# Two weight tiles moved ahead of the last head's products, branch tiles split by GpSimd alone, and output loads under an order block

## The chip, the cores and the metric

The kernel runs on one core of a Trainium2 chip. The time is the device time of one execution in microseconds; the kernel before took 1817.15 us (median of three runs, 1814.82 to 1818.39). One execution was taken by the hardware profiler; its trace is the source of every other time.

The core has five engines, each with its own queue that it works off in order: TensorE (PE, with its weight loads PEld), VectorE (DVE), ScalarE (ACT), GpSimd (POOL) and SyncE (SP, which here only issues transfers). An instruction that waits for a semaphore holds up all that stands behind it on its engine.

## What is computed

Two layers of a small transformer with adaptive norms: 256 tokens of width 2048 (and 256 context tokens) go through a Fourier mixing layer and then an attention layer, whose branch is 4096 wide. The change lies in the second layer, from its attention on:

```python
def _attention_branch(h, hc, w_in, sink, rows, cols, need_ctx):
    q, k, v, z = jnp.split(h @ w_in, [D_BRANCH, D_BRANCH + kvw, D_BRANCH + 2 * kvw], axis=-1)
    ...
    o = lax.map(block, ...)          # softmax(q k + mask, sink) v, 64 heads on 8 key heads
    ...
    y = jnp.moveaxis(o, 0, 1).reshape(b, n, D_BRANCH) * jax.nn.silu(z)
...
    x = x + gate * (y @ w_out[i])
    ...
return _rmsnorm(x, final_g)
```

## The kernel before

Products are done in split single precision: a matrix is kept as a rounded high part and the low rest, and one product is three TensorE instructions, high by high, high by low, low by high (`mm3`, lines 78 to 80). So every weight tile that is loaded (`raw`, 1 MB, three buffers, on SP's queue, line 49) is split before use: ScalarE casts the high part (line 65), VectorE subtracts it from the tile (line 66), in halves of 1024 columns (`half_split`; six buffers).

**Heads and weight units.** The attention stage is one loop over i = 0 to 65. Step i issues the scores of head i (`stage_s`, lines 1154 and 1155; 64 heads, two blocks of 128 tokens each), one weight unit (`filler`), the value product of head i − 2 (`stage_o`, lines 1176 and 1177) and a second weight unit. A weight unit is half of a 1 MB tile or of a query tile: queries of later heads ("q"), gates ("z", 32 of them in two halves, lines 1118 and 1120), and last, 12 units "o" of the output product.

After the scores, VectorE adds the mask and takes the row maximum (line 1156), ScalarE the exponential (line 1159), and the softmax is written as an fp16 pair `f` by ScalarE and VectorE (lines 1166, 1167; three buffers). Two DMA transposes on SP's queue (line 1168) turn it into `ft`, which the value product reads. ScalarE and VectorE take the result out of PSUM (lines 1182, 1183), and `emit_y` multiplies it by the gate (line 1139) into `y1`, 32 branch blocks of 256 columns (half a tile each).

**The output product.** `y @ w_out` is done in three parts by columns: 512 columns (`oA`, weights `wo1a`, 16 half tiles), 1024 (`wo1b`, 16 tiles) and 512 (`wo1c`). Before it can be used, a branch block is split into high and low like the weights (`y_split`): ScalarE casts, and for blocks 0 to 23 GpSimd subtracts, for blocks 24 to 31 VectorE. Blocks 0 to 15 are written into the buffers of the layer's input `hx1`, which are free once the last z unit has read them, 16 to 23 into `act` buffers, and 24 to 31 into a pool `fin`, which opens when the attention's pool has closed. `o1_step` does two token blocks of one branch block, calling `y_split` up to four blocks ahead. The 12 "o" units cover blocks 0 to 23 of the first part; blocks 24 to 31 follow after the loop, then part two with its own four PSUM banks, then part three.

**The output's inputs.** After the loop GpSimd's queue (line 1223 on) loads the gate `gbc` (1 MB), the residual `x2` out of the scratch tensor `x1d` (eight pieces of 256 KB) and the final gain `fg` (1 MB). `evac` (lines 1239 to 1244) needs them when part one is complete.

**What sets the order.** The instructions are written in program order, and a scheduler reorders each engine's queue at build time by its own estimate of durations; the pools and semaphores are added by the same build. `tc.issue_after(ins)` adds order edges to `ins` from those instructions of its block that are on the engine of `ins`; it adds no wait.

Of the kernel before, what the change touches and what calls it, by code (L numbers as in the profile page):

```python
# [31 lines left out]
def tile_dit(ctx: ExitStack, tc: tile.TileContext, a: dict, out: bass.AP):  # L32
# [10 lines left out]
    def psum():  # L43
        return pp.tile([P, 512], F32, tag="ps", name="ps")
# [842 lines left out]
    with tc.tile_pool(name="h1", reuse_waits="tile", bufs=16) as h1p:  # L887
# [72 lines left out]

        y1 = []
        raw1, fin = [None], []
        oA, kg1, yh = [], [0], []
        with tc.tile_pool(name="at", reuse_waits="tile", bufs=2) as at:

            kk, qq, obs, szs = {}, {}, {}, {}
# [113 lines left out]
            def emit_unit():  # L1080
                if pos[0] >= len(ulist):
                    return
                u = ulist[pos[0]]
                if pos[0] not in ready:
                    ready[pos[0]] = prep(u)
                if pos[0] + 1 < len(ulist):
                    ready[pos[0] + 1] = prep(ulist[pos[0] + 1])
                w = ready.pop(pos[0])
                pos[0] += 1
                kind, n, i, o = u  # L1090
                if kind == "o":
                    if n == 0:
                        oA.extend([psum(), psum()])
                    for j in range(2):
                        o1_step(n * 2 + j, oA, *(t[:, j * 512 : (j + 1) * 512] for t in w))
                    return
                wh, wl = w
                if kind == "q":
                    if i == 0:
                        o += [psum(), psum()]  # L1100
                    if (n, i) == (0, 4):
                        with tc.issue_after(last_cast[0]):
                            prep_kk(0)
                    for j in range(2):
                        k = i * 2 + j
                        q = slice(j * 512, (j + 1) * 512)
                        for tb in range(2):
                            mm3(o[tb], hx1[k][:, tb * P : (tb + 1) * P], hx1[k][:, N + tb * P : N + (tb + 1) * P], wh[:, q], wl[:, q], k == 0, k == KT - 1)
                    if i == 7:
                        finish_q(n, o)  # L1110
                else:
                    if i == 0:
                        o.append(psum())
                    for k in range(i * 8, i * 8 + 8):
                        q = slice((k % 8) * P, (k % 8 + 1) * P)
                        for part in (0, 1) if k < KT - 1 else (1, 0):
                            if part == 0:
                                PE.matmul(o[0], wh[:, q], hx1[k], start=k == 0, stop=k == KT - 1)  # L1118
                            else:
                                PE.matmul(o[0][:, 0:N], wl[:, q], hx1[k][:, 0:N], start=False, stop=False)  # L1120
                    if i == 1:
                        th = at.tile([P, N], F32, tag="th", name="th", bufs=3)
                        zs = at.tile([P, N], F32, tag="zs", name="zs", bufs=1)
                        S.copy(zs, o[0][:, N : 2 * N])
                        V.tensor_tensor(zs, o[0][:, 0:N], zs, op=ALU.add)
                        S.activation(th, zs, AF.Tanh, scale=0.5)
                        V.scalar_tensor_tensor(th, th, 1.0, zs, op0=ALU.add, op1=ALU.mult)
                        szs[n] = th
                        emit_y(n)
# [3 lines left out]
            def emit_y(blk):  # L1133
                if blk not in szs or (blk, 1) not in obs or blk in ydone:
                    return
                ydone.add(blk)
                if blk % 2 == 0:
                    y1.append(act())
                V.scalar_tensor_tensor(y1[blk // 2][:, (blk % 2) * N : (blk % 2 + 1) * N], obs[blk, 1], dsc[:, blk // 4 : blk // 4 + 1], szs.pop(blk), op0=ALU.mult, op1=ALU.mult)

            def stage_s(i):
                hk, blk, hh = i // 8, i // 2, i % 2
# [21 lines left out]
                for tb in range(2):  # L1164
                    f = at.tile([P, 1024], F16, tag="f", name="f", bufs=3)
                    S.activation(f[:, 0:512], pt[tb], AF.Copy, scale=sm[:, tb : tb + 1])  # L1166
                    V.scalar_tensor_tensor(f[:, 512:1024], pt[tb], sm[:, tb : tb + 1], f[:, 0:512], op0=ALU.mult, op1=ALU.subtract)  # L1167
                    nc.sync.dma_start_transpose(ft[:, :, tb, :], f)
                return ft

            def stage_o(i, ft):
# [36 lines left out]
            for i in range(66):  # L1208
# [11 lines left out]
        with tc.tile_pool(name="fin", reuse_waits="tile", bufs=1) as fp:  # L1220
            fin.append(fp)
            gbc = fp.tile([P, D], F32, name="gbc")
            nc.gpsimd.dma_start(gbc, gated.broadcast_to([P, D]))
            x2 = []
            for tb in range(2):
                x2.append([act() for _ in range(4)])
                for c in range(4):
                    nc.gpsimd.dma_start(x2[tb][c], x1d[tb, :, c * 512 : (c + 1) * 512])
            fg = fp.tile([P, D], F32, name="fg")
            nc.gpsimd.dma_start(fg, a["fg"].broadcast_to([P, D]))  # L1230
            ss = fp.tile([P, 9], F32, name="ss")

            sum_end = [None]
# [15 lines left out]
                    o1_step(k + i, oA, *(t[:, i * 512 : (i + 1) * 512] for t in w))  # L1249
            for tb in range(2):  # L1250
                evac(tb, 0, oA[tb])
            o = [[psum() for _ in range(2)] for _ in range(2)]
            for kg in range(16):
                w = ws_split(raw(a["wo1b"][kg]))
                for j in range(2):
                    k = kg * 2 + j
                    wh, wl = w[j]
                    for tb in range(2):
                        for c in range(2):
                            q = slice(c * 512, (c + 1) * 512)  # L1260
                            mm3(o[tb][c], yh[k][:, tb * P : (tb + 1) * P], yh[k][:, N + tb * P : N + (tb + 1) * P], wh[:, q], wl[:, q], k == 0, k == NB - 1)
# [173 lines left out]
```

## Time and profile before

| | |
|---|---|
| median of three runs | 1817.15 us |
| profiled execution | 1817.29 us |
| its span | 1815.5 us |
| TensorE busy | 1768.6 us (97%) |
| VectorE busy | 1412.0 us (78%) |
| ScalarE busy | 896.9 us (49%) |
| GpSimd busy | 212.4 us (12%) |
| mean granted TensorE clock | 0.993 |
| attention stage, first value product to last | 1172 to 1659 us |

How to read the rows further down: a row of the time order has start, duration, engine, line, operation, result `<-` operands and count, and in brackets how long the engine stood idle before it and what ended that. A row of a group has count, busy time, mean nanoseconds of one, and idle time before. Matmuls are pipelined, so their durations overlap; the distance of two starts is what one costs. Shares over the whole span average over stages with different limits.

### The profile page before, as it was taken

What the parts mean: (1) busy time and instruction counts of PE and PEld (TensorE: products, weight loads), DVE (VectorE), ACT (ScalarE), POOL (GpSimd) and SP (SyncE); (2) the same over time, 40 slices, a digit from 0 to 9 for tenths busy, and PEclk for the clock granted to TensorE, in tenths of its full rate; (3) what the DMA queues carried; (4) which work ended last, traced back from release to release, by engine and by line L of the source; (5) the groups of instructions that cost most, each with busy time, mean ns of one, the idle gap of its engine ahead of it and who ended that gap; (6) DMA issues with size and microseconds to landing.
All of it is one profiled execution on the core that took longest, in us unless ns stands there. A gap on an engine that the chain in (4) does not pass through costs nothing. (4 is left out here: it accounts for less than half of the span.)

```text
span 1815.5 us, 25987 instructions
## 1 busy us (share of the span) xinstructions
PE 1768.6 (97%) x9417; PEld 1480.2 (82%) x9417; DVE 1412.0 (78%) x2759; ACT 896.9 (49%) x1540; POOL 212.4 (12%) x213
## 2 busy tenths in 40 slices
PE   6999999999999999999999999999999999997998
PEld 4679999888888888888888888788878888875886
DVE  5679888786878887776875654899999999985455
ACT  5545454532222233324322534687778888874343
POOL 0001122100000000000001000402302231161001
PEclk9999999999999999999999999999999999998999
DMA  9988889665767647663567323587988888986553
GB/s 395 417 331 234 231 239 255 216 228 224 252 228 262 244 168 295 229 237 121 186 230 293 119 93 116 162 206 196 224 203 195 215 223 211 213 219 194 188 182 139
DMA packets 209472, 399.91 MB, mean 220 GB/s; under 512 B 156288, under 2 KB 156688, under 8 KB 174272
## 3 DMA queue, kind: packets, MB, share of 16 engines
q1 hardware_dynamic: 185280, 360.24, 61.7%
q0 software_dynamic: 19920, 31.06, 7.0%
q10 hardware_dynamic: 4144, 6.95, 1.1%
q8 instruction: 74, 1.21, 0.3%
q14 instruction: 54, 0.44, 0.1%
HBM read 352.06 MB, written 12.59 MB: 201 GB/s over the span
## 5 line engine op out<-in xcount | busy, mean ns | idle before, releaser
L65 ACT CAST wh<-raw 128x1024 fp32r<-128x1024 f32 x333 | 348.7, 1048 | 531.9 <-PE ps L79 431.1
L66 DVE TENSOR_TENSOR wl<-raw,wh 128x1024 fp32r<-128x1024 f32 x333 | 430.5, 1296 | 220.1 <-ACT wh L65 217.7
L79 PE MATMUL ps<-act,wh 128*128 128x512 f32 x1024 | 398.2, 389 | 0.0
L78 PE MATMUL ps<-act,wh 128*128 128x512 f32 x1024 | 393.8, 389 | 0.0
L80 PE MATMUL ps<-act,wl 128*128 128x512 f32 x1024 | 392.9, 389 | 0.0
L80 PEld LDWEIGHTS ps<-act,wl 128*128 128x128 f32 x1024 | 192.3, 188 | 39.8
L79 PEld LDWEIGHTS ps<-act,wh 128*128 128x128 f32 x1024 | 192.3, 188 | 39.8
L78 PEld LDWEIGHTS ps<-act,wh 128*128 128x128 f32 x1024 | 192.3, 188 | 39.7
L1118 PE MATMUL ps<-h,wh 128*128 128x512 f32 x512 | 185.5, 398 | 0.0
L686 DVE CUSTOM_DVE_ANT_0 raw<-raw,cb 128x512 f32<-128x512 f32 x256 | 172.4, 688 | 11.6 <-DMA raw<-in_adw 8.0
L686 DVE CUSTOM_DVE_ANT_0 junk<-raw,cb 128x512 f32<-128x512 f32 x192 | 131.8, 686 | 32.8 <-DMA raw<-in_adw 21.9
L1120 PE MATMUL ps<-h,wl 128*128 128x256 f32 x512 | 138.9, 281 | 0.0
L79 PE MATMUL ps<-wl,h 128*128 128x512 f32 x320 | 127.1, 397 | 0.4 <-DVE wl L66 0.4
L80 PE MATMUL ps<-wh,h 128*128 128x512 f32 x320 | 125.3, 395 | 0.0
L78 PE MATMUL ps<-wh,h 128*128 128x512 f32 x320 | 124.0, 402 | 0.0
L1167 DVE SCALAR_TENSOR_TENSOR f<-p,sm,f 128x512 f16<-128x512 f32 x128 | 102.9, 821 | 16.4 <-ACT f L1166 16.0
L1118 PEld LDWEIGHTS ps<-h,wh 128*128 128x128 f32 x512 | 96.6, 189 | 19.1
L1166 ACT ACTIVATE f<-p,sm 128x512 f16<-128x512 f32 x128 | 88.1, 717 | 41.5 <-DMA ft<-f 21.6
L1159 ACT ACTIVATE p<-ps,mx 128x512 f32<-128x512 f32 x128 | 87.9, 688 | 38.1 <-DVE mx L1156 31.6
L1120 PEld LDWEIGHTS ps<-h,wl 128*128 128x128 f32 x512 | 97.0, 190 | 2.8
L1156 DVE CUSTOM_DVE_ANT_0 ps<-ps,mask,nsink 128x512 f32<-128x512 f32 x128 | 93.4, 749 | 1.8 <-PE ps L1155 1.6
L1176 PE MATMUL ps<-ft,v 128*128 128x256 f16 x256 | 60.6, 277 | 19.7 <-DMA ft<-f 19.3
(334 smaller groups left out, 3394.9 us busy)
## 6 DMA issues: line engine op xcount, KB each, us to landing
raw<-in_wz SPq DMA_DIRECT2D x64, 1024.0 KB, 5.5
raw<-in_adw SPq DMA_DIRECT2D x64, 1024.0 KB, 5.2
raw<-in_awp SPq DMA_DIRECT2D x32, 1024.0 KB, 12.8
raw<-in_wo SPq DMA_DIRECT2D x32, 1024.0 KB, 6.1
raw<-in_wq SPq DMA_DIRECT2D x32, 1024.0 KB, 5.3
raw<-in_wu SPq DMA_DIRECT2D x32, 1016.0 KB, 6.2
raw<-in_wo1b SPq DMA_DIRECT2D x16, 1024.0 KB, 4.9
act<-in_xT POOLq DMA_DIRECT2D x32, 256.0 KB, 6.3
```

Source lines behind the costliest of these rows:

```text
L65: last_cast[0] = S.copy(h, src).ins
L66: last_sub[0] = eng.tensor_tensor(l, src, h.bitcast(F32), op=ALU.subtract).ins
L78: PE.matmul(o, wh, xh, start=start, stop=False)
L79: PE.matmul(o, wh, xl, start=False, stop=False)
L80: return PE.matmul(o, wl, xh, start=False, stop=stop).ins
L686: V.tensor_tensor_reduce(junk if s == 0 and i < 3 else wf, wf, cb[:, s, kq * 512 : kq * 512 + 512], 1.0, 0.0, ALU.mult, ALU.add, acc[:, i, ...
L1118: PE.matmul(o[0], wh[:, q], hx1[k], start=k == 0, stop=k == KT - 1)
L1120: PE.matmul(o[0][:, 0:N], wl[:, q], hx1[k][:, 0:N], start=False, stop=False)
L1156: V.tensor_tensor_reduce(o, o, mask[:, tb, :], -0.125, nsink[:, i : i + 1], ALU.add, ALU.min, mx[:, tb : tb + 1])
L1159: S.activation(pt[tb], so[tb], AF.Exp, bias=mx[:, tb : tb + 1], scale=-1.0, accum_out=sm[:, tb : tb + 1])
L1166: S.activation(f[:, 0:512], pt[tb], AF.Copy, scale=sm[:, tb : tb + 1])
L1167: V.scalar_tensor_tensor(f[:, 512:1024], pt[tb], sm[:, tb : tb + 1], f[:, 0:512], op0=ALU.mult, op1=ALU.subtract)
```

## The change

It has four edits. (1) `b_steps(kg)` holds the inner loop of part two; at i = 65, between the two filler calls (which are empty there) and ahead of that step's value product, the first two of its 16 tiles are issued, and the rest start at tile 2 in the old place. (2) One more filler is called at i = 2, so that each later unit comes one place earlier. (3) For blocks 0 to 23 the split is a copy and a subtraction on GpSimd, without ScalarE; the buffers of blocks 0 to 7 are `act` ones and 8 to 23 take those of `hx1`; and two blocks are split at each half of z units 30 and 31. (4) The loads of `x2`, `gbc` and `fg` stand in `tc.issue_after(turn_end[0])`, the last transpose, and `x2` is loaded in another order.

```diff
             def y_split(k):
-                if 16 <= k < 24:
+                if k < 8:
                     t = act(F32R)
                 else:
-                    t = (h1p if k < 16 else fin[0]).tile([P, 512], F32R, tag="h1" if k < 16 else "ys", name="ys", bufs=16)
-                split(t[:, 0:N], t[:, N : 2 * N], y1[k // 2][:, (k % 2) * N : (k % 2 + 1) * N], GP if k < 24 else V)
+                    t = (h1p if k < 24 else fin[0]).tile([P, 512], F32R, tag="h1" if k < 24 else "ys", name="ys", bufs=16)
+                src = y1[k // 2][:, (k % 2) * N : (k % 2 + 1) * N]
+                if k < 24:
+                    GP.tensor_copy(t[:, 0:N], src)
+                    GP.tensor_tensor(t[:, N : 2 * N], src, t[:, 0:N].bitcast(F32), op=ALU.subtract)
+                else:
+                    split(t[:, 0:N], t[:, N : 2 * N], src)
                 yh.append(t)
...
+            def b_steps(kg):
+                w = ws_split(raw(a["wo1b"][kg]))
+                for j in range(2):
+                    k = kg * 2 + j
+                    wh, wl = w[j]
+                    for tb in range(2):
+                        for c in range(2):
+                            q = slice(c * 512, (c + 1) * 512)
+                            mm3(oB[tb][c], yh[k][:, tb * P : (tb + 1) * P], yh[k][:, N + tb * P : N + (tb + 1) * P], wh[:, q], wl[:, q], k == 0, k == NB - 1)
...
+                    if n >= 30:
+                        for _ in range(2):
+                            y_split(len(yh))
...
-                    nc.sync.dma_start_transpose(ft[:, :, tb, :], f)
+                    turn_end[0] = nc.sync.dma_start_transpose(ft[:, :, tb, :], f).ins
...
                 filler()
+                if i == 2:
+                    filler()
+                if i == 65:
+                    oB.extend([psum() for _ in range(2)] for _ in range(2))
+                    for kg in range(2):
+                        b_steps(kg)
                 if i >= 2:
                     stage_o(i - 2, pts.pop(i - 2))
                 filler()
...
-            nc.gpsimd.dma_start(gbc, gated.broadcast_to([P, D]))
...
+            with tc.issue_after(turn_end[0]):
+                nc.gpsimd.dma_start(gbc, gated.broadcast_to([P, D]))
                 for c in range(4):
-                    nc.gpsimd.dma_start(x2[tb][c], x1d[tb, :, c * 512 : (c + 1) * 512])
-            fg = fp.tile([P, D], F32, name="fg")
-            nc.gpsimd.dma_start(fg, a["fg"].broadcast_to([P, D]))
+                    for tb in range(2):
+                        nc.gpsimd.dma_start(x2[tb][c], x1d[tb, :, c * 512 : (c + 1) * 512])
+                nc.gpsimd.dma_start(fg, a["fg"].broadcast_to([P, D]))
...
-            o = [[psum() for _ in range(2)] for _ in range(2)]
-            for kg in range(16):
-                w = ws_split(raw(a["wo1b"][kg]))
...
+            for kg in range(2, 16):
+                b_steps(kg)
             for tb in range(2):
                 for c in range(2):
-                    evac(tb, 1 + c, o[tb][c])
+                    evac(tb, 1 + c, oB[tb][c])
```

More of the change, by code (lines that the diff above doesn't have):

```diff
@@ L1222, in tile_dit @@
             gbc = fp.tile([P, D], F32, name="gbc")
[L1223 to L1226, printed above, removed]
+            fg = fp.tile([P, D], F32, name="fg")
+            x2 = [[act() for _ in range(4)] for _ in range(2)]
+            with tc.issue_after(turn_end[0]):
+                nc.gpsimd.dma_start(gbc, gated.broadcast_to([P, D]))
                 for c in range(4):
-                    nc.gpsimd.dma_start(x2[tb][c], x1d[tb, :, c * 512 : (c + 1) * 512])
-            fg = fp.tile([P, D], F32, name="fg")
-            nc.gpsimd.dma_start(fg, a["fg"].broadcast_to([P, D]))
+                    for tb in range(2):
+                        nc.gpsimd.dma_start(x2[tb][c], x1d[tb, :, c * 512 : (c + 1) * 512])
+                nc.gpsimd.dma_start(fg, a["fg"].broadcast_to([P, D]))
             ss = fp.tile([P, 9], F32, name="ss")
```

10 lines of the change are left out of this document (2 added, 8 removed).

## The prediction

> **What bounds the kernel now.** I read the page first, then the busy time by stretches, the chain of work that ended last, and the order of time on each engine around the end of the attention stage. The page gives the span and says what the attention's value products (line 1176) wait for; the stretches say where TensorE stands still.
>
> ```profile
> span 1815.5 us, 25987 instructions
> L1176 PE MATMUL ps<-ft,v 128*128 128x256 f16 x256 | 60.6, 277 | 19.7 <-DMA ft<-f 19.3
> ```
> ```profile
> 1600.00:1620.00 20.00, 20.00 (x100) 15.86 (x99) 19.91 (x32) 17.06 (x39) 19.99 (x23) 1.00 0.80 211
> 1620.00:1640.00 20.00, 16.61 (x74) 13.03 (x73) 12.65 (x26) 11.31 (x23) 0.42 (x1) 0.91 1.11 267
> 1640.00:1660.00 20.00, 7.14 (x36) 5.25 (x35) 7.25 (x9) 5.40 (x11) 3.42 (x5) 0.68 0.92 229
> ```
>
> (Columns of the second: stretch, length, busy time of PE, PEld, DVE, ACT, POOL, granted clock, DMA share, GB/s.) TensorE is full up to about 1625 and loses over 16 us in the next 35, with VectorE at 19.91 of 20 just ahead. The chain of waits runs through the transposes of the softmax (`ft<-f`) there:
>
> ```profile
> 1627.28 7.79 DMA ft<-f
> ...
> 1643.70 13.69 DMA ft<-f
> ```
>
> I number the 64 head passes i: S(i) their scores (lines 1154, 1155), T(i) their two transposes, O(i) the value product. In order of time TensorE reads:
>
> ```profile
> 1583.73 0.40 PE L1155 MATMUL ps<-kkl,qb 128*128 128x512 f32 x1
> 1601.52 0.28 PE L1176 MATMUL ps<-ft,v 128*128 128x256 f16 x1
> 1605.88 0.39 PE L1155 MATMUL ps<-kkl,qa 128*128 128x512 f32 x1
> 1624.20 0.40 PE L80 MATMUL ps<-wh,ys 128*128 128x512 f32 x1
> 1625.37 0.39 PE L79 MATMUL ps<-wl,ys 128*128 128x512 f32 x1
> 1629.14 0.28 PE L1176 MATMUL ps<-ft,v 128*128 128x256 f16 x1 [3.39 <-DMA ft<-f]
> 1633.25 0.59 PE L78 MATMUL ps<-wh,act 128*128 128x512 f32 x1
> 1644.19 0.40 PE L79 MATMUL ps<-wl,act 128*128 128x512 f32 x1
> 1657.44 0.40 PE L1176 MATMUL ps<-ft,v 128*128 128x256 f16 x1 [12.86 <-DMA ft<-f]
> 1661.82 0.39 PE L78 MATMUL ps<-wh,ys 128*128 128x512 f32 x1
> ```
>
> From 1624.20 to 1625.37 are five products: 0.234 each at full pace. O(60) starts at 1629.14, 3.5 us after the product before it should have given way (1625.60); the 8 narrow (0.11) and 8 wide products to 1633.25 then take 4.1 instead of 2.7, so 1.4 is lost to the lower clock. O(63) comes 13.0 late (1644.42 to 1657.44), and the 8 and 8 after it take 4.4 instead of 2.7: 1.6. Together **19.5 us** in which TensorE could have worked. Everything after 1662 is full until the closing stretch, and the change leaves that alone. So a change here is worth at most 19.5 us of 1817.3.
>
> **The change part by part.**
>
> *Work ahead of O(63).* Before, four wide products stand between O(62) and O(63) in the built order; after, 40 (the first two tiles of the output's second part; the other 8 of their 48 go right behind O(63)'s first product). 36 × 0.234 = 8.4 us of cover are moved there. Counted over the built order, TensorE's work from the end of S(63) to O(63) rises from 11.1 to 19.4 us (76 × 0.234 + 16 × 0.11). For O(57) to O(62) it is 15.1, 17.5, 17.6, 17.6, 17.6, 16.6, against 17.6, 17.6, 18.0, 19.4, 18.5, 16.6 before, since the extra filler at i = 2 puts every weight unit one place ahead of the heads. A pass that lands later than that stops TensorE.
>
> *How late a pass lands.* S(57) ends at 1584.1 and O(57) starts unhindered at 1601.52: 17.4 or less. S(60) ends at 1606.1 and O(60) waits until 1629.14: 23.0. S(63) ends at 1633.25, O(63) starts at 1657.44: 24.2. Two things made the difference, loads from POOL and VectorE slowed by POOL:
>
> ```profile
> 1593.83 15.52 POOL L66 TENSOR_TENSOR ys<-act,ys 128x256 fp32r<-128x256 f32 x15 [0.70 <-ACT ys L65]
> 1609.36 7.29 POOL L66 TENSOR_TENSOR act<-act 128x256 fp32r<-128x256 f32 x6
> 1616.60 3.82 POOL L1228 DMA_DIRECT2D act<-x1d  x7
> ...
> 1645.69 0.56 POOL L1223 DMA_DIRECT2D gbc<-gated  x1
> 1646.25 0.54 POOL L1230 DMA_DIRECT2D fg<-in_fg  x1
> ```
> ```profile
> 1619.89 6.57 SPq L1168 DMA_TRANSPOSE ft<-f  x2
> ...
> 1642.37 4.87 SPq L1168 DMA_TRANSPOSE ft<-f  x2
> ```
> ```profile
> gbc<-gated POOLq DMA_DIRECT2D x1, 1024.0 KB, 12.7
> fg<-in_fg POOLq DMA_DIRECT2D x1, 1024.0 KB, 16.4
> ft<-f SPq DMA_TRANSPOSE x12, 6.1
> ```
>
> T(60) is issued into seven loads of 256 KB, T(63) into two of 1 MB; a transpose usually lands in 6.1, T(63) took 13.69.
>
> *The held loads.* The block that is to hold them orders only instructions of its anchor's engine. The anchor is a transpose on SP, the loads are POOL's: in the built program they carry no wait for a transpose. They stand behind POOL's last subtraction, all eight x1d loads first; gbc waits for S(63)'s last product, fg only for work long done and a queue slot. So x1d goes out when POOL has finished splitting, and gbc and fg (2 MB) right after S(63), some 9 us before T(63) (1633.25 to 1642.37) instead of 3 behind it. I cost this edit at a displacement: the collision leaves T(63) and falls on T(61) and T(62).
>
> *The split on GpSimd alone.* Each of 24 blocks now takes a copy and a subtraction on POOL, no ScalarE cast.
>
> ```profile
> L65 ACT CAST ys<-act x24: 393/403/411, 1591.9 to 1662.6; 128x256 fp32r<-128x256 f32 x24
> L66 POOL TENSOR_TENSOR ys<-act,ys x16: 727/741/1727, 1592.4 to 1608.6; 128x256 fp32r<-128x256 f32 x16
> 1547.14 2.98 POOL L885 TENSOR_TENSOR act<-act,rt 128x512 f32<-128x512 f32 x2
> ```
>
> ScalarE is rid of 24 casts (the 16 ys ones of this list's 24 and 8 into act tiles), at most 24 × 0.40 = 9.7 us; VectorE, not ScalarE, was full there, so I count nothing. No row shows a POOL copy. Bounds: half the quickest subtraction (0.36, one input instead of two) and the slowest subtraction (1.73); I take 0.75, the median subtraction, as the nearest form. Subtractions come to 1.1 each (22.8 us for 21). By the built waits the first eight blocks depend only on old results, so they run behind the rope work that ends at 1550; the other 16 wait for the last z unit, as before (1592). 16 × (0.75 + 1.1) = 30 us: x1d goes out at about 1622, with the heads one filler (2.8 us) later than before, so T(60) meets it as it did. At the bounds it is 1615 and 1637; from 1602, where the last z unit gives way to O(57), two blocks take 3.7 us (half the 7.4 between passes: S(57) to S(60) is 22.15 for three), so TensorE needs block 12 by 1624 and block 23 by about 1643, and POOL itself is late by 1 us at the upper one.
>
> VectorE pays for POOL's work:
>
> ```profile
> L66 DVE TENSOR_TENSOR wl<-raw,wh 128x1024 fp32r<-128x1024 f32 x9 | 11.0, 1220 | 0.8 <-ACT wh L65 0.7
> ...
> L66 DVE TENSOR_TENSOR wl<-raw,wh 128x1024 fp32r<-128x1024 f32 x6 | 10.1, 1694 | 0.7 <-ACT wh L65 0.7
> L1167 DVE SCALAR_TENSOR_TENSOR f<-p,sm,f 128x512 f16<-128x512 f32 x4 | 4.1, 1037 | 0.0
> ```
>
> The first row is 1560 to 1592 (POOL idle), the others 1594 to 1616 (POOL full). Six splits cost 0.47 more each, four f 0.29 (0.75 without POOL), with small forms some 5 to 6 us in 22: 0.25 us per us of POOL. Subtractions stay 24; 24 copies add 18 us of POOL, so 0 to 4.5 us of VectorE lag, half of it already at 1550 to 1565. I take 1.1 net at O(60).
>
> The Trainium skill speaks against this part: its "GPSIMD Engine Reference" (§ 4.1 Engine selection) calls the engine about half as fast as VectorE on two inputs but roughly line rate on one, and § 8 Key points has it contend with VectorE instructions of two SBUF inputs. The two-input `wl` rows above agree; no run here shows the copy. At line rate (an estimate from that page, about 0.3) x1d would go out near 1615, the lower bound.
>
> *Behind O(63).* Before, eight products of blocks 22 and 23 hid the last block's split; after, block 24 is next.
>
> ```profile
> 1659.37 0.37 ACT L1182 COPY ot<-ps 64x256 f32<-64x256 f32 x1 [14.57 <-PE ps L1177]
> 1659.64 0.40 ACT L65 CAST ys<-act 128x256 fp32r<-128x256 f32 x1
> ```
>
> The cast stands behind that copy on ScalarE: 0.3 + 0.4 after O(63) ends, 0.8 with the start of the product. In front of the copy now stands a cast of the last wo1a tile, whose load goes out behind T(63): up to 1.5 us more if O(63) was late. I take 1.1.
>
> **The sum.** Removed 19.5. Left or new: O(60) 23.0 − 17.6 = 5.4, and 1.1 for VectorE; 1.0 at O(62) and O(63) (T(63) relieved to 6 to 8 us brings 24.2 to about 18, under 19.4; T(62) later by about 5, of which O(60)'s own stop pays); 1.5 for the low clock after the stop; 1.1 behind O(63). That is 10.1, a gain of 9.4. The profiled execution took 1817.29 (span and 1.8 around it), the median 1817.15: **1807.7 us**.
>
> **The rivals.**
>
> *Nearly all of it is won.* The copy is quick, x1d falls between transposes, no pass exceeds 17.4: 1817.2 − 19.5 + 0.8 = 1798.5. For it: 17.4 fits in 17.5 to 19.4. Against: O(57) has 15.1, and the DMA share is already 0.80 in the stretch to 1620.
>
> *The hold does nothing and no gain is left.* x1d costs O(60) 5.4, gbc and fg cost O(62) the 13.69 − 6.1 = 7.6 that they cost T(63), two low clocks 3.0, VectorE's full 4.5 reaches the path, 1.1 behind: 21.6 left of 19.5: 1819. For it: all 4 MB still come before T(63). Against: stops ahead of O(62) give later passes time, so the terms hardly add.
>
> *Slower: weight loads ahead of transposes on SP.* The filler at i = 2 makes SP's order two loads in a row ahead of a transpose pair once in each of seven groups of eight passes. If the second waits for its buffer, the pair, its O and TensorE are late by up to one unit (3.7): 7 × 3.7 − 9.4 = 16.5 slower, 1834. From 1.3 us a group the gain is gone. Against: by the built waits each load's VectorE instruction precedes the transposes', so SP seldom waits in the wrong order, and the cover per pass is 17.1 to 20.7.
>
> **Chances.** Forecast (1803 to 1812) 0.50; nearly all 0.20; no gain 0.18; slower 0.12. The range takes the first two and most of the third: 1798 to 1817. A measurement of this kernel can tell 0.2% (3.6 us): faster is below 1813.5, with 0.50 + 0.20 + 0.02 = 0.72; slower above 1820.8, 0.12 and a little of the third, 0.14; same 0.14.
>
> **What would show it.** Right: no wait over 2 us at the last O; a stop of 4 to 8 us at one of O(57) to O(60) with x1d loads in flight; gbc issued right behind S(63), ahead of the last transposes; `wl` near 1.7 us wherever POOL copies. Wrong: x1d behind the last transposes; a POOL copy outside 0.36 to 1.73; TensorE waiting for POOL; stops at O every eight passes from 1180 on.

## The result, and the profile after

| | before | after |
|---|---|---|
| median (runs) | 1817.8 us (6) | 1827.8 us (6) |
| lowest to highest | 1812.2 to 1819.4 | 1823.1 to 1829.1 |
| profiled execution / its span | 1817.3 / 1815.5 us | 1829.1 / 1827.3 us |
| TensorE stops from 1200 us to the end of the attention stage and just behind it | 17.0 us | 25.9 us |

The ratio is 1.0055 with a 95% interval of 1.0042 to 1.0067: the kernel became 10 us slower, where the prediction said 9.4 us faster with a range of 1798 to 1817.

First the order of time on TensorE after the change (start, duration, engine, line, operation; in brackets the idle time before it and what ended it). O is now line 1196, S lines 1174 and 1175.

```profile
1338.24 0.28 PE L1196 MATMUL ps<-ft,v 128*128 128x256 f16 x1 [1.73 <-DMA ft<-f]
1399.60 0.28 PE L1196 MATMUL ps<-ft,v 128*128 128x256 f16 x1 [1.13 <-DMA ft<-f]
1462.32 0.28 PE L1196 MATMUL ps<-ft,v 128*128 128x256 f16 x1 [1.67 <-DMA ft<-f]
1527.24 0.39 PE L1196 MATMUL ps<-ft,v 128*128 128x256 f16 x1 [2.94 <-DMA ft<-f]
1591.18 0.37 PE L1196 MATMUL ps<-ft,v 128*128 128x256 f16 x1 [5.39 <-DMA ft<-f]
1653.65 0.40 PE L1196 MATMUL ps<-ft,v 128*128 128x256 f16 x1 [8.73 <-DMA ft<-f]
1659.55 0.40 PE L1175 MATMUL ps<-kkl,qb 128*128 128x512 f32 x1
1679.04 0.28 PE L1196 MATMUL ps<-ft,v 128*128 128x256 f16 x1
1682.75 0.50 PE L78 MATMUL ps<-wh,ys 128*128 128x512 f32 x1 [0.82 <-ACT ys L65]
1684.63 0.73 PE L80 MATMUL ps<-wh,ys 128*128 128x512 f32 x2 [0.68 <-DVE ys L66]
```

The last S ends at 1659.95 and O(63) starts at 1679.04 without a bracket: the 12.9 us in front of it are gone. In their place O(60) waits 8.73 instead of 3.39, O(53) waits 5.39 where it waited for nothing, and O(21), O(29), O(37) and O(45), each 61 to 65 us behind the one before, wait 1.1 to 2.9. The groups of the two kernels between 1180 and 1560 us, a stretch in which hardly an edit but the extra unit acts (GpSimd's first copies start at 1558.7), say the same (count, busy time, mean ns, idle time before and its causes); first before, then after:

```profile
L1176 PE MATMUL ps<-ft,v 128*128 128x256 f16 x204 | 47.7, 275 | 1.4 <-DMA ft<-f 1.1 <-ACT f L1166 0.4
```
```profile
L1196 PE MATMUL ps<-ft,v 128*128 128x256 f16 x196 | 46.6, 277 | 11.0 <-DMA ft<-f 10.2 <-ACT zs L1142 0.7
```

The busy times by stretches (PE, PEld, DVE, ACT, POOL, granted clock, DMA share, GB/s) show the two largest stops with the lower clock that follows them, and GpSimd at work between:

```profile
1580.00:1600.00 20.00, 14.61 (x73) 12.10 (x73) 17.45 (x36) 15.09 (x32) 0.00 (x0) 0.83 0.85 184
...
1620.00:1640.00 20.00, 20.00 (x101) 15.81 (x100) 19.88 (x30) 12.41 (x26) 20.00 (x25) 1.00 0.73 188
1640.00:1660.00 20.00, 11.27 (x47) 8.66 (x46) 10.50 (x20) 9.36 (x17) 0.57 (x2) 0.83 1.09 215
```

What happens in front of O(60) stands in the time order of GpSimd, then of SP's queue, then in the chain of work that ended last (start, duration, what), then in the time order of ScalarE:

```profile
1609.40 4.65 POOL L983 CAST ys<-act 128x256 fp32r<-128x256 f32 x8 [38.06 <-PE ps L1135]
...
1636.22 4.35 POOL L1255 DMA_DIRECT2D act<-x1d  x8
...
1660.93 0.54 POOL L1252 DMA_DIRECT2D gbc<-gated  x1 [20.36 <-DVE mx L1176]
```
```profile
1636.89 3.92 SPq L1188 DMA_TRANSPOSE ft<-f  x2
1640.91 0.60 SPq L49 DMA_DIRECT2D raw<-in_wo1b  x1
1643.19 12.60 SPq L1188 DMA_TRANSPOSE ft<-f  x2
1655.91 0.50 SPq L49 DMA_DIRECT2D raw<-in_wo1b  x1
```
```profile
1638.23 15.38 DMA ft<-f
```
```profile
1653.71 0.72 ACT L1186 ACTIVATE f<-p,sm 128x512 f16<-128x512 f32 x1 [3.08 <-DMA ft<-f]
1656.94 0.72 ACT L1186 ACTIVATE f<-p,sm 128x512 f16<-128x512 f32 x1 [2.51 <-DMA ft<-f]
```

GpSimd's splits end at 1636 and its next instructions are the eight loads of x1d. They are not held by anything: the last transposes go out 30 us later. The pair issued at 1636.89 is T(60). With the loads of x1d and a weight tile in flight, its second transpose, issued at 1638.23, lands after 15.38 us, and O(60) starts right behind it. The pair issued from 1643 on, T(61), stretches over 12.60 us. ScalarE's bracket shows why a late transpose delays a later pass as well: `f` has three buffers, and the `f` of pass 62 at 1653.71 waits until the transpose that landed at 1653.61 has read one of them. gbc goes out at 1660.93, right behind the last S.

### The profile page after: what moved, and what is told of

It is laid out like the page before. It is cut to its first block, busy times and chain, and to the rows that moved or that the text cites. A ratio compares the mean times of both kernels' runs of the same rounds, so it can differ in the third digit from the quotient of the medians.

```text
span 1827.3 us, 25927 instructions
## 1 busy us (share of the span) xinstructions
PE 1771.3 (97%) x9417; PEld 1481.2 (81%) x9417; DVE 1425.7 (78%) x2759; ACT 889.2 (49%) x1516; POOL 229.6 (13%) x237
## 3 DMA queue, kind: packets, MB, share of 16 engines
q10 hardware_dynamic: 4144, 6.95, 1.1%
## 5 line engine op out<-in xcount | busy, mean ns | idle before, releaser
L1187 DVE SCALAR_TENSOR_TENSOR f<-p,sm,f 128x512 f16<-128x512 f32 x128 | 108.0, 869 | 18.1 <-ACT f L1186 17.8
L1133 PEld LDWEIGHTS ps<-h,wh 128*128 128x128 f32 x512 | 97.5, 190 | 19.4
```

## The experiments

All times are medians, with the ratio to the kernel before measured on the same chip. "Stops" are TensorE's idle times in the trace; "1200 to 1560" is the part of the attention stage ahead of the splits.

| run | what is changed | us | ratio, interval | stops 1200 to 1560 | at O(60) / O(62) / O(63) |
|---|---|---|---|---|---|
| before | | 1817.8 | | 0.8 | 3.4 / 0 / 12.9 |
| after | all four edits | 1827.8 | 1.0055 (1.0042 to 1.0067) | 10.2 | 8.7 / 0 / 0 |
| e1 | extra unit alone | 1829.5 | 1.0066 (1.0050 to 1.0083) | 10.3 | 3.3 / 5.2 / 1.8 |
| e2 | after, no extra unit | 1818.4 | 1.0007 (0.9990 to 1.0023) | 1.5 | 9.2 / 2.7 / 0 |
| e3 | cover alone | 1813.2 | 0.9979 (0.9968 to 0.9990) | 1.1 | 4.1 / 0 / 5.9 |
| e4 | after, cast back on ScalarE | 1826.2 | 1.0047 (1.0030 to 1.0064) | 10.3 | 4.5 at O(59) / 3.7 / 0 |
| e5 | two extra units alone | 1833.8 | 1.0102 (1.0080 to 1.0124) | 13.3 | 3.7 / 15.8 / 2.5 |
| e6 | cover, loads held | 1803.7 | 0.9929 (0.9913 to 0.9944) | 1.2 | 0 / 1.1 / 0 |
| e7 | after, no unit, loads held | 1806.4 | 0.9943 (0.9927 to 0.9958) | 0.2 | 0 / 1.5 / 0 |
| e8 | loads held, alone | 1802.4 | 0.9918 (0.9903 to 0.9934) | 1.0 | 0 / 0.7 / 1.3 |
| e9 | e1, query turn one slot later | 1842.7 | 1.0136 (1.0117 to 1.0155) | 15.2 | 4.1 / 4.2 / 1.9 |
| e10 | e5, query turn two slots later | 1825.5 | 1.0045 (1.0032 to 1.0058) | 8.3 | 6.0 / 6.4 / 2.5 |
| e11 | after, loads held | 1820.2 | 1.0014 (1.0003 to 1.0024) | 9.8 | 0 / 0 / 0 |
| e12 | e8 with the loads on GpSimd's queue | 1804.6 | 0.9934 (0.9920 to 0.9948) | 0.8 | 0 / 0.6 / 1.2 |
| e13 | e1 without the queries' low halves | 1823.4 | 1.0037 (1.0024 to 1.0049) | 3.9 | 7.2 / 4.5 / 1.9 |
| e14 | e1, weight loads tied to transposes | 1867.8 | 1.0284 (1.0266 to 1.0303) | 23.4, most of it at the weights | 0 (6.3 at O(59)) / 6.2 / 2.5 |

### The edits one at a time: e1 to e4

**e1, the extra unit alone**, on the kernel before:

```diff
                 filler()
+                if i == 2:
+                    filler()
                 if i >= 2:
```

> The kernel before with one edit of the change, the extra weight unit at i = 2. In the changed kernel TensorE stood for 13.0 us at value products before 1560 us, against 3.8 before, nearly all of it at one pass in every eight (21, 29, 37, 45), and 5.4 more at O(53). Theory A (the extra unit shifts the weight loads and VectorE's work against the heads by half a pass, and one pass in eight lands late): the same stops appear here without any other edit, 9 us if O(53) needs the GpSimd split as well and up to 15 if it does not; O(60) and O(63) keep about their 16 us; 1826 to 1833, ratio 1.005 to 1.008. Theory B (the stops come from GpSimd's copies and the loads at the end): no new stops before 1560, 1815 to 1820, ratio 0.998 to 1.002.

1829.5 us, 11.4 more than before. The group of O between 1180 and 1560 has the idle time of the whole change:

```profile
L1176 PE MATMUL ps<-ft,v 128*128 128x256 f16 x195 | 46.3, 277 | 10.8 <-DMA ft<-f 10.7
```

The stops stand in front of the same passes (1.76 at O(21), 0.97, 1.77 and 2.96 at the next three, 3.27 at O(53)), and no other edit is in the kernel. Together 13.6 us (two expectations further down say 14.1). So theory A holds, and the loss ahead of 1560 belongs to the extra unit. What the split adds to O(53) is 2.1 (5.39 against 3.27; with the cast back on ScalarE, e4, it is 3.16).

**e2, the change without the extra unit:**

```diff
                 filler()
-                if i == 2:
-                    filler()
                 if i == 65:
```

> The changed kernel without the extra weight unit at i = 2; all other edits stay. Theory A: the stops at every eighth pass go back to the 3.8 us of the kernel before, O(53) loses most of its 5.4; against the 1827.8 of the changed kernel 9 to 15 us less: 1812 to 1819, ratio to the kernel before 0.997 to 1.001, and what is left of the loss sits at O(60). Theory B (GpSimd's eight early copies and subtractions slow VectorE and cause O(53)'s stop): O(53) still stops for 4 us or more, 1818 to 1821. If neither the unit nor the split is the cause, 1825 to 1829.

1818.4 us: 9.5 less than the whole change, and level with the kernel before; its twelve runs spread from 1812.7 to 1828.4. O(53) does not stop; a `wl` that is 1.08 late stops TensorE at 1571 instead. The large stops that are left stand at O(60) and O(62) (the expectation of e7 calls the second O(63)):

```profile
1635.53 0.39 PE L1196 MATMUL ps<-ft,v 128*128 128x256 f16 x1 [9.23 <-DMA ft<-f]
1654.21 0.28 PE L1196 MATMUL ps<-ft,v 128*128 128x256 f16 x1 [2.70 <-DMA ft<-f]
```

Theory A holds for the regular stops, and B falls for O(53). But the three other edits together win nothing.

**e3, the cover alone** on the kernel before (the same `b_steps`, called for two tiles at i = 65 and for the other 14 after the loop):

```diff
                 filler()
+                if i == 65:
+                    oB.extend([psum() for _ in range(2)] for _ in range(2))
+                    for kg in range(2):
+                        b_steps(kg)
                 if i >= 2:
...
-            for kg in range(16):
+            for kg in range(2, 16):
```

> The kernel before with one edit of the change, the first two tiles of the output's second part ahead of O(63); no extra unit, split by ScalarE and GpSimd as before, loads where they were. If the cover does what the prediction said, O(63)'s stop falls from 12.9 to 4 or less, the 8.4 us are won and a little of the low clock: 1807 to 1811, ratio 0.994 to 0.996. Rival: the two weight tiles' loads (2 MB) now stand ahead of T(62) and T(63) and make them later by what the cover gives, or the work behind O(63) has to wait for the last split: 1814 to 1818, ratio 0.998 to 1.000.

1813.2 us, 4.9 less than before: between the two expectations. In this build 28 wide products stand between O(62) and O(63), 24 more than before (24 × 0.234 = 5.6 us); O(63)'s stop falls by 6.95 and does not vanish: its second transpose takes 13.53 us to land, as it took 13.69 before. O(60) waits 4.14:

```profile
1628.94 0.40 PE L1186 MATMUL ps<-ft,v 128*128 128x256 f16 x1 [4.14 <-DMA ft<-f]
1657.07 0.37 PE L1186 MATMUL ps<-ft,v 128*128 128x256 f16 x1 [5.91 <-DMA ft<-f]
```

**e4, the change with the high half of the 24 blocks cast by ScalarE again:**

```diff
-                if k < 24:
-                    GP.tensor_copy(t[:, 0:N], src)
-                    GP.tensor_tensor(t[:, N : 2 * N], src, t[:, 0:N].bitcast(F32), op=ALU.subtract)
-                else:
-                    split(t[:, 0:N], t[:, N : 2 * N], src)
+                split(t[:, 0:N], t[:, N : 2 * N], src, GP if k < 24 else V)
```

> The changed kernel with the first half of each of the 24 splits back as a ScalarE cast (the subtraction stays on GpSimd); all other edits stay, the early emission of eight blocks too. Theory B (GpSimd's 24 copies slow VectorE, hold back f and cause the stops of 5.4 at O(53) and 8.7 at O(60)): O(53) under 2, O(60) 3 to 5, 1814 to 1820. Theory A (the stops come from the shifted order, and from loads that meet the transposes): O(53) 3 to 5.4, the loads from GpSimd's queue some 14 us earlier in time against the heads, the stop moves to O(58) or O(59) but stays; 1824 to 1829.

1826.2 us, 1.6 less than the whole change, which the two intervals can't tell apart. O(53) waits 3.16 instead of 5.39; the 8.73 at O(60) becomes 4.50 at O(59) and 3.74 at O(62). GpSimd's copies move the place of the stop at the end and hardly its size. Theory A was right again.

### The hold: e6, e7, e8, e11, e12

In e8 the only difference from the kernel before that changes an order is where the loads of x1d, gbc and fg stand, with their order among themselves; e6 is the same with the cover of e3, e7 and e11 have it in the changed kernel without and with the extra unit:

```diff
-            nc.gpsimd.dma_start(gbc, gated.broadcast_to([P, D]))
...
+            with tc.issue_after(turn_end[0]):
+                nc.sync.dma_start(gbc, gated.broadcast_to([P, D]))
                 for c in range(4):
-                    nc.gpsimd.dma_start(x2[tb][c], x1d[tb, :, c * 512 : (c + 1) * 512])
+                    for tb in range(2):
+                        nc.sync.dma_start(x2[tb][c], x1d[tb, :, c * 512 : (c + 1) * 512])
+                nc.sync.dma_start(fg, a["fg"].broadcast_to([P, D]))
```

Now the loads are on the queue of the transpose that anchors them, so the order block acts.

> The cover alone (1813.2: stops of 4.1 at O(60) and 5.9 at O(63) left) with the loads of x1d, gbc and fg moved to SP behind the last transpose, so that they are truly held. Theory C (loads in flight with the last transposes make them late): O(60) under 1.5, O(63) under 2, and with the low clocks gone 1802 to 1807. Rival D (the passes are late by themselves, from VectorE and from the weight loads, which stay): both stops stay within 2 us of theirs, 1811 to 1814. Rival E (the held loads come too late for the closing work or push back the weight tiles behind them): the stops vanish but TensorE waits for weights or PSUM after 1670: 1810 to 1820.

> The changed kernel without the extra unit, with the same loads truly held on SP: cover, GpSimd's copies and a real hold. Without the hold it took 1818.4, with stops of 9.2 at O(60) and 2.7 at O(63). Theory C (the loads, which GpSimd's longer work moved into the transposes of pass 60): O(60) under 2, O(63) under 1; 1804 to 1809. Theory B (GpSimd's copies themselves slow VectorE and with it f): O(60) 4 or more, 1811 to 1816. The difference to the cover with held loads is then the price of the split by GpSimd alone.

> The kernel before with the loads of x1d, gbc and fg on SP behind the last transpose, no cover, no other edit. Theory C: O(60) falls from 3.4 to under 1; T(63) lands in 6 to 8 us instead of 13.7, so O(63) falls from 12.9 to 6 to 8; 1808 to 1812. Rival D: O(60) 3 and O(63) 11 to 13 stay, 1816 to 1819.

e6 took 1803.7, e7 1806.4, e8 1802.4 us: theory C in all three, and O(60) does not wait in any of them. e8 is also faster than both kernels of this study. The hold alone wins 15 us, more than any expectation said (C had 1808 to 1812 for e8), and of the 16.3 us at O(60) and O(63) there are 2.0 left, at O(62) and O(63). The granted clock, 0.91 and 0.68 from 1620 to 1660 in the kernel before, is 1.00 there. TensorE in e8 at O(62) and O(63), then SP's queue, then the chain:

```profile
1638.14 0.28 PE L1188 MATMUL ps<-ft,v 128*128 128x256 f16 x1 [0.74 <-DMA ft<-f]
...
1644.72 0.28 PE L1188 MATMUL ps<-ft,v 128*128 128x256 f16 x1 [1.25 <-DMA ft<-f]
```
```profile
1637.27 5.38 SPq L1180 DMA_TRANSPOSE ft<-f  x2
1642.75 4.15 SPq L1241 DMA_DIRECT2D act<-x1d  x8
```
```profile
1638.93 5.74 DMA ft<-f
```

From the end of the last S (1628.3 here) to O(63) are 16.4 us, where the kernel before needed 24.0 (24.2 by the prediction's count). The landing of the second transpose accounts for it: 5.74 us here, 13.69 before, with a weight load 0.7 us ahead of the pair in both. So the pass was not late by itself: the loads in flight made it late. With the hold there is little left to cover, and the cover then costs a little (e6 is 1.3 us above e8, 1803.1 to 1806.1 against 1801.2 to 1803.2): in e6 TensorE waits 1.92 and 0.79 behind O(63) for the split of block 24, as the prediction said of this edit, in e8 0.77. GpSimd's split costs some 2.7 us (e7 against e6; their runs overlap); TensorE waits 1.85 for a `wl` at 1570 there, in the stretch of the eight early blocks, and 2.72 behind O(63).

> The changed kernel with one thing mended: its loads of x1d, gbc and fg go out on SP behind the last transpose. If the two losses are independent (the extra unit 9.5 to 12 us, the loads that were not held 12 to 14), 1814 to 1819, with no stop over 2 us after O(53) and the stops at one pass in eight as in the changed kernel. If the late passes of the extra unit make the end worse in any case: O(60) still 4 or more, 1820 to 1826.

1820.2 us: 7.7 less than the changed kernel, a little above the range. No O after O(53) waits, and the passes up to O(53) wait as in the changed kernel (9.8 and 5.08). The second transpose of T(60), 15.38 us in the changed kernel, lands in 3.1. But behind O(63) TensorE waits 3.78 for the split of block 24, which the expectation left out. The extra unit costs 13.8 us here (against e7), 9.5 without the hold (the change against e2) and 11.4 by itself.

**e12** asks whether it is the time of the loads or the queue that issues them. They stay on GpSimd, behind a copy of one column of the last transposed tile:

```diff
+            see = at.tile([P, 1], F16, tag="see", name="see", bufs=1)
+            turned = GP.tensor_copy(see, ft_last[0][:, 7, 1, 0:1]).ins
...
+            with tc.issue_after(turned):
                 nc.gpsimd.dma_start(gbc, gated.broadcast_to([P, D]))
```

> The kernel before with its loads of x1d, gbc and fg kept on GpSimd's queue, behind a one-column copy that reads the last transposed tile: held by data, on the old queue. On SP the held loads took 1802.4. Theory H (it is when the loads go out): 1801 to 1806, O(60) and O(63) under 2. Rival I (it is the queue: transfers issued by GpSimd disturb the transposes and those issued by SP do not, or GpSimd's issuing slows VectorE): 1810 to 1816, with a stop behind O(63) in place of the one at it.

```profile
1644.73 0.72 POOL L1232 COPY see<-ft 128x1 f16<-128x1 f16 x1 [2.49 <-DMA ft<-f]
1645.39 4.35 POOL L1244 DMA_DIRECT2D act<-x1d  x8
```

1804.6 us: the copy waits for the transpose and the loads go out behind it, with 12.9 of the 15.3 us; the intervals of the two runs overlap. It is when they go out. In both, x1d arrives in time for the closing work: TensorE is full from 1660 to 1700.

### Why one unit ahead costs 11 us: e5, e9, e10, e13, e14

The prediction's rival had SP's order as the mechanism: two weight loads in a row ahead of a pair of transposes. e1 has that order at the late pass. VectorE before the change, at pass 21 (its S ends at 1312.0), then SP:

```profile
1324.05 0.75 DVE L1167 SCALAR_TENSOR_TENSOR f<-p,sm,f 128x512 f16<-128x512 f32 x1
...
1325.11 0.75 DVE L1156 CUSTOM_DVE_ANT_0 ps<-ps,mask,nsink 128x512 f32<-128x512 f32 x1
...
1325.78 0.74 DVE L1167 SCALAR_TENSOR_TENSOR f<-p,sm,f 128x512 f16<-128x512 f32 x1
1326.44 1.22 DVE L66 TENSOR_TENSOR wl<-raw,wh 128x1024 fp32r<-128x1024 f32 x1
```
```profile
1321.24 0.34 SPq L49 DMA_DIRECT2D raw<-in_wq  x1
1324.87 2.92 SPq L1168 DMA_TRANSPOSE ft<-f  x2
```

and the same in e1:

```profile
1326.33 0.75 DVE L1156 CUSTOM_DVE_ANT_0 ps<-ps,mask,nsink 128x512 f32<-128x512 f32 x1
...
1327.67 1.22 DVE L66 TENSOR_TENSOR wl<-raw,wh 128x1024 fp32r<-128x1024 f32 x1
1328.80 1.41 DVE L1167 SCALAR_TENSOR_TENSOR f<-p,sm,f 128x512 f16<-128x512 f32 x2
```
```profile
1321.14 8.10 SPq L49 DMA_DIRECT2D raw<-in_wq  x2
1329.62 5.07 SPq L1168 DMA_TRANSPOSE ft<-f  x2
```

Before, the `f` of the late pass came between the two reductions of the next and ahead of a `wl`; in e1 it comes behind both reductions and the `wl`, and the second weight load, which waits for that `wl`, goes out right ahead of the transposes. From the end of S to the end of f are 14.5 us before and 16.0 in e1, from there to O 3.6 and 6.6. So both steps became longer, and the second is the landing of the transposes. The pair of pass 21 in the view of the tile `ft` (us from issue to landing), before and in e1:

```profile
DMA to landing us min/median/max: 3.0/3.1/3.1
```
```profile
DMA to landing us min/median/max: 5.7/5.9/6.2
```

Before, the weight load in front goes out 3.6 us ahead of the pair, in e1 0.7. It is the same at the other late passes (O(29), O(37), O(45), O(53)): the second transpose lands in 5.7 to 7.4 us instead of 3.1, and `f` is 0.5 to 2.9 later. At four of the five the longer landing (2.6 to 4.4) is more than the whole stop, at O(53) it is 2.8 of 3.27. SP's wait for the buffer, the rival's mechanism, holds nothing up: at all five the load goes out when that `wl` ends, while VectorE works on the first `f`, and the first transpose follows 0.07 us behind that `f`. So the one `wl` ahead of the `f` does two things: it makes `f` later, and it releases a load right ahead of the pair.

**e5**, two extra units (`filler()` twice at i = 2), on the kernel before:

> The kernel before with two extra weight units at i = 2 instead of one, a whole pass of the heads ahead instead of half a pass. The one extra unit alone took 1829.5 against 1818.1, with stops of 14.1 us at value products from 1280 to 1560 and at O(53). Theory A1 (it is the half pass: a weight unit's VectorE work changes its place between a pass's reductions and its f, so that f comes behind one more wl): with a whole pass the old order comes back, stops between 1200 and 1600 under 2 us in sum, and the time differs only by the end, where four slots of cover are empty instead of two: 1816 to 1823. Theory A2 (any unit ahead of the heads makes every pass later, since the buffers and VectorE run closer): stops at one pass in eight of the same size or larger, 1828 to 1836.

1833.8 us. In this build SP's queue is one load, then one pair of transposes, throughout, and the loss is larger (part of it at the end, where O(62) waits 15.8; the profile is that of the longest run, 1842.6). O waits 8.2 us between 1180 and 1560, products wait another 5 for `wl`:

```profile
L1176 PE MATMUL ps<-ft,v 128*128 128x256 f16 x196 | 45.8, 274 | 8.2 <-DMA ft<-f 8.1
```

So two loads in a row are not needed for a loss, and it is not the half pass (A1) either. The late passes are other ones (20, 28, 36, 44, 52). Their transposes land in 3.1 us; it is `f` that ends 17.6 to 18.0 us behind S, where it took 8.3 to 11.1 at these passes before.

**e9 and e10** put the turn of the next group's queries, which comes four times 0.69 us of VectorE's work per group, back to the pass at which it stood before; the threshold 2 becomes 3 in e1 and 4 in e5:

```diff
-                if defer and defer[0][0] + 2 < j:
+                if defer and defer[0][0] + 3 < j:
```

> One extra unit as in the first experiment (1829.5), but the turn of the next group's queries (four transposes on TensorE, two casts and two subtractions for each half) is taken one slot later, so that it stands against the heads where it stood before. Theory Q (the lead brings the query turn and its VectorE work to a pass where VectorE is already behind): the stops at one pass in eight fall to under half of 14.1 us, 1818 to 1824. Theory U (it is the weight units' own lead, whatever the turn does): the stops stay above 10 us, 1826 to 1832.

> Two extra units (1833.8), with the query turn two slots later, where it stood against the heads before. In the two-unit kernel SP's order is one weight load, then one pair of transposes, all the way, as in the kernel before, and it lost 16 us all the same, so two loads in a row on SP are not needed for the loss. Theory Q: stops between 1200 and 1600 fall from 16 to under 6 us, 1820 to 1826. Theory U: they stay above 10, 1830 to 1836.

e10 won 8.3 us against e5 and still loses 8.1 against the kernel before; its time is theory Q's, its stops from 1200 to 1600 (10.1) are theory U's. e9 lost 13 against e1, outside both ranges, with runs from 1835.6 to 1846.3 (the profile is that of the shortest). The place of the query turn matters, but putting it back does not undo the loss.

**e13** takes the work away instead: the two subtractions of each query turn are left out, GpSimd writes zeros, so the queries' low halves are missing from the scores.

```diff
-                V.tensor_tensor(qa[64:128, :], o[0:64, :], qa[0:64, :].bitcast(F32), op=ALU.subtract)
-                V.tensor_tensor(qb[0:64, :], o[64:128, :], qb[64:128, :].bitcast(F32), op=ALU.subtract)
+                GP.memset(qa[64:128, :].bitcast(F32), 0.0)
+                GP.memset(qb[0:64, :].bitcast(F32), 0.0)
```

> The one extra unit alone (1829.5), with the low halves of the turned queries left out: VectorE's two subtractions of each query turn (0.69 us each, four in a group of eight passes, 2.8 us) are replaced by GpSimd writing zeros. Theory V (the stops come from VectorE, which is busy for some 55 of 60 us and has the query subtractions to do just where the passes are late): the stops at one pass in eight go, under 4 us in sum from 1200 to 1600; 1816 to 1820. Theory L (they come from the shifted weight loads on SP and their transfers): stops over 9 us remain, 1826 to 1831.

```profile
L1176 PE MATMUL ps<-ft,v 128*128 128x256 f16 x200 | 47.4, 275 | 4.5 <-ACT p L1159 2.0 <-DMA ft<-f 1.2 <-ACT ot L1182 0.7
```

The waits for transposes in this stretch fall from 10.7 to 1.2, and all stops of O from 10.8 to 4.5. The time, 1823.4, is above the expectation because the end became worse than in e1: 13.6 us at O(60), O(62) and O(63) for 10.3, with the loads not held. In this build SP's order is also one load per pair, 2.9 us or more ahead of it at passes 16 to 52, and the second transposes land in 3.0 to 3.9. So e13 took away both the later `f` (11.2 us behind S at pass 21, 16.0 in e1) and the longer landing, and does not tell VectorE from SP. That a late `f` is enough for stops, e5 shows.

**e14** was to give SP that order in e1 with VectorE's work all there, by tying each weight load to the transposes of an earlier pass:

```diff
+                    if len(turn_end) >= 3:
+                        with tc.issue_after(turn_end[-3]):
+                            raws1[src] = raw(w)
+                    else:
+                        raws1[src] = raw(w)
```

> The one extra unit alone, with each weight load held behind the transposes of the third pass before the unit's own, which gives SP one load and one pair of transposes in turn through the heads, as in the kernel before; VectorE's work is all there. Theory L: the stops at one pass in eight go, 1816 to 1821. Theory V: stops of 9 us or more in sum from 1200 to 1600 remain, 1826 to 1834.

1867.8 us, outside both ranges, and inconclusive: the loads now come too late, and TensorE waits for weights once in each group, which hides what the passes would do.

```profile
1352.16 0.74 PE L78 MATMUL ps<-wh,h 128*128 128x512 f32 x2 [2.77 <-ACT wh L65]
```

## Why the prediction was wrong

*The step that failed first: the extra filler at i = 2.* In the sum it costs nothing; as a rival it has 0.12, with a price "up to one unit (3.7)" per group and "from 1.3 us a group the gain is gone". Stops from 1200 to 1560 and at O(53) are 15.6 us in the changed kernel against 0.8, and e1 puts 11.4 us of time on this edit alone. Stops at O every eight passes, one of the prediction's own signs of being wrong, are the first rows above. The place (one pass in eight, all through the stage) was the rival's, and the size lay within its bound. Its mechanism was half right: the weight load does stand right ahead of the pair at these passes in e1, but it costs by a longer landing (5.7 to 7.4 us for 3.1), not by SP waiting for a buffer, and a later `f` comes with it; e5 loses by the later `f` without it. What counted against it, "the cover per pass is 17.1 to 20.7", was a true count of TensorE's work and the wrong thing to ask. The pass became later at the same time, with VectorE's and SP's built orders changed: from the end of S(21) to O(21) are 22.6 us in e1, where it took 18.1 before. The prediction used the built order on TensorE to count cover and did not compare the built order on VectorE, which is busy 55 to 58 of every 60 us there, nor how far the weight loads stand ahead of the transposes on SP.

*The second: the end as a whole.* The sum removed 19.5 and left 10.1. e2, which is the change without the extra unit, measures this part: 1818.4, no gain. That is the rival "the hold does nothing and no gain is left" (1819, 0.18), in its time and in its cause; its terms cancelled by luck, for it had 5.4 at O(60) and 7.6 at O(62), where e2 has 9.2 and 2.7. Term by term:

- Ahead of O(63): right. From the end of S(63) to O(63) 19.1 us pass without a stop in the changed kernel, 19.4 were counted (its terms add to 19.5), and T(63) lands in 6.4 to 8.0 where 6 to 8 were taken. The cover alone (e3) won 4.9 us, with a smaller cover than the change's.
- The hold: right that it holds nothing, that x1d goes out behind the last subtraction and that gbc follows the last S. The time of x1d was 1636 instead of 1622, 27 us behind the last z unit where 30 were counted; that unit gave way later because of the stops ahead. Costing it as "a displacement" was the wrong size: O(60) waits 8.7 (9.2 in e2), 5.4 and 1.1 were left in the sum.
- What the sum did not ask is what the kernel would take with those loads out of the way. The prediction named them as one of two reasons for the lateness of O(60) and O(63), and then set out to cover passes of 23 to 24 us. e8 shows a last pass of 16.4 and a kernel at 1802.4 with no cover at all, 15 of the 19.5 us. The row was in the prediction: a transpose that "usually lands in 6.1" took 13.69.
- The split on GpSimd: the copy was mis-sized little (0.724 median for 0.75 taken, 0.396 to 1.386 for bounds of 0.36 to 1.73), GpSimd's total for 16 blocks was 27 for 30.

```profile
L983 POOL CAST ys<-act x16: 396/724/1386, 1609.4 to 1627.5; 128x256 fp32r<-128x256 f32 x16
...
L983 POOL CAST act<-act x8: 395/505/1397, 1558.7 to 1563.2; 128x256 fp32r<-128x256 f32 x8
```

  The estimate from the Trainium skill, "GPSIMD Engine Reference" (§ 4.1 Engine selection), about 0.3 at line rate, lies below the fastest of these copies; the trace does not agree with it for copies that run beside VectorE's work (VectorE is busy 19.88 of 20 us from 1620 on). The price of the edit, some 2.7 us by e7 against e6, is more than the 1.1 that the sum gave it at O(60), and lies elsewhere: 1.85 at a `wl` at 1570, and 0.8 more than in e6 behind O(63).
- Behind O(63): 1.1 taken, 1.5 measured (0.82 and 0.68).

*The third is how the rivals were weighed.* Two of them came true together: no gain at the end, and 10 us at the passes. As exclusive cases with 0.18 and 0.12 they left no chance for the two together, and the range ended at 1817, below the 1819 of the one it was to take in for the most part. They rest on different edits and different stretches, so the case of both should have had a chance of its own.

*What stays open.* That an extra unit costs 8 to 25 us in e1, e5, e9, e10 and the changed kernel is shown, and that the stops from 1200 to 1560 fall from 10.3 to 3.9 when VectorE has 2.8 us less to do per group and, in the same build, no weight load goes out right ahead of a pair. The rows of e1 give the later `f` and the longer landing their lengths, and the landing is the longer of the two at most passes; but no run took one away and left the other (e14 was to), so how the time divides between them is not settled. The stops account for 8.9 of the 11.8 us between the two profiled spans; the rest fits the lower clock behind the new stops (0.83 in two stretches of 20 us) and was not worked out.

## What to carry to other kernels

When a wait in front of a product ends with a transfer, ask first why the transfer is late, and only then how to hide it: taking 4 MB of loads out of its way won 15 us, hiding it won 5. An order block binds only the queue of its anchor, so a load that is to stay behind a transfer must be on that transfer's queue or behind an instruction that reads its result. And where two engines run near full, shifting one stream of work against another by a single unit changes the built order on all queues: compare VectorE's and SP's order, not only TensorE's.

## What the runs showed of the hardware that was not expected

- Loads in flight lengthened the landing of a transpose, up to five times: the second of T(60) took 15.38 us with x1d in flight and 3.1 with the loads held (the changed kernel and e11). It goes the same way with a single weight load: in the kernel before, e1 and e13, passes 16 to 52, the second transpose took 3.5 to 7.4 us (median 5.0, 45 pairs) where a weight load went out less than 1.8 us ahead of the pair, and 3.0 to 4.4 (median 3.1, 61 pairs) where it was more than 2.7.
- The delay is handed on through the three `f` buffers: between 1600 and 1690 us ScalarE's `f` waited 7.1 us for transposes before, 2.8 in e8.

```profile
L1166 ACT ACTIVATE f<-p,sm 128x512 f16<-128x512 f32 x10 | 6.9, 718 | 8.1 <-DMA ft<-f 7.1 <-ACT p L1159 0.9
```
```profile
L1178 ACT ACTIVATE f<-p,sm 128x512 f16<-128x512 f32 x10 | 7.0, 718 | 4.4 <-DMA ft<-f 2.8 <-issue 1.3
```

- It made little difference whether SP or GpSimd issues the held loads: 1802.4 and 1804.6 us, with overlapping intervals.
